# Softmax-minus-one-hot backward: two transfer queues, loads by row or whole block and stores by row, against one queue in a fixed order with even and odd partitions

## The chip, the cores and the metric

The kernel runs on one core of a Trainium2 chip. The metric is the device time of one execution in microseconds (us); the time before is the median of three runs. Logits, labels and the result lie in the chip's main memory (HBM); all arithmetic works on the on-chip memory, which has 128 partitions. Sixteen DMA engines of the core carry data between the two. A transfer (a DMA) is issued by the instruction stream of one engine, here SyncE (SP) or ScalarE (ACT), and goes into that engine's queue; both queues feed the same sixteen DMA engines.

## The reference

The work is the gradient of a cross-entropy loss for 8192 rows of 8192 float32 logits:

```python
logits_max = np.max(logits, axis=-1, keepdims=True)
exp_logits = np.exp(logits - logits_max)
softmax = exp_logits / np.sum(exp_logits, axis=-1, keepdims=True)
one_hot[batch_idx, seq_idx, labels] = 1.0
return (softmax - one_hot).astype(np.float32)
```

Each logit is read once and each result written once: 268.44 MB in and 268.44 MB out.

## The kernel before

**Tiling.** The 8192 rows are cut into 32 blocks of 256 rows. In a block, partition p holds the two neighbouring rows 2p and 2p+1, so what a partition holds of a block is one run of 64 KB in HBM. The first index, j = 0 or 1, of a partition's two rows makes a "row" in the language of the code: row t = 2b + j is the 128x8192 tile of 4 MB with one matrix row per partition. There are 64 such tiles. The buffer `X` has three slots of two tiles each, 8 MB a slot; block b lies in slot b mod 3, and the load of block b+3 must wait until the stores of block b have left the slot.

**Compute.** For each tile, `row_max` lets VectorE (DVE) take the negated maximum of each partition; ScalarE (ACT) computes exp(x - max) in place and sums it; DVE takes the reciprocal of the sum; ACT scales the tile by it; DVE subtracts 1 where a column number (`iota`, held in the matmul memory) equals the label. The order on DVE is written out by hand and staggered by one tile: maximum of tile t+1, then the subtraction of tile t. `finished[t]` names the semaphore count that says that tile t is done. Only the last tile is scaled and subtracted in two halves of 4096 columns.

**Forms of a transfer.** The table `PIECES` names three: "r" moves one tile (128 partitions, one 32 KB run each), "w" a whole block (128 partitions, 64 KB runs), "h" half a block: the 64 even partitions, then the 64 odd ones, both tiles of each, 64 KB runs. The strings `LOADS` and `STORES` choose a form for each block. Before, loads are "r" for blocks 0 to 4 and 26 to 31 and "w" for the 21 blocks between; all stores are "r". "h" is not used. Every helper `run` call records one instruction, so that nearly all instructions stand under line 68 in the profile.

**Order.** `load(b)` issues block b's loads on SP's queue, each waiting for those stores of block b-3 that share its bytes (`meets`); the calls stand in the loop over tiles, one block ahead of the maxima. The last tile of the first three blocks also waits until the column numbers, first made in its place, have been copied away. `store(t)` issues the store of tile t on ACT's queue, after the exponential of tile t+1 and ahead of the scaling of tile t+1. So loads and stores sit in two queues, and each DMA engine has packets of both to serve. At the end ACT waits for the last stores.

Of the kernel before, what the change touches and what calls it, by code (L numbers as in the profile page):

```python
# [8 lines left out]
G = 2  # L9
SLOTS = 3  # L10


LOADS = "rrrrrwwwwwwwwwwwwwwwwwwwwwrrrrrr"
STORES = "rrrrrrrrrrrrrrrrrrrrrrrrrrrrrrrr"


@with_exitstack
def kernel(
    ctx: ExitStack,
    tc: tile.TileContext,  # L20
    logits: bass.AP,
    labels: bass.AP,
    out: bass.AP,
):
    nc = tc.nc
    fp32 = mybir.dt.float32
    i32 = mybir.dt.int32
    i16 = mybir.dt.int16
    Act = mybir.ActivationFunctionType
    Alu = mybir.AluOpType  # L30

    x_nv = logits.flatten_outer_dims()
    o_nv = out.flatten_outer_dims()
    N, V = x_nv.shape
    T = N // P
    B = T // G
    lab_bp = labels.rearrange("a b -> (a b)").rearrange("(b q) -> b q", q=G * P)
    x_b = x_nv.rearrange("(b p j) v -> b p j v", p=P, j=G)
    o_b = o_nv.rearrange("(b p j) v -> b p j v", p=P, j=G)

    const = ctx.enter_context(tc.tile_pool(name="const", bufs=1))
    psum = ctx.enter_context(tc.tile_pool(name="psum", bufs=1, space=bass.MemoryType.PSUM))


    X = const.tile([P, SLOTS, G, V], fp32)
    lab_raw = const.tile([B, G * P], labels.dtype)
    lab_f = const.tile([B, G, P], fp32)
    ident = const.tile([B, B], fp32)
    lab = const.tile([P, G, B], fp32)

    m, s, r = (const.tile([P, T], fp32, name=n) for n in ("m", "s", "r"))

    iota = psum.tile([P, V], i16)
    lab_ps = iota[:].bitcast(fp32)[:, :T].rearrange("p (j b) -> p j b", j=G)

    with tc.tile_critical():  # L56
        sem = tc.alloc_semaphore
        got = [[sem(f"got{i}{q}") for q in range(2)] for i in range(SLOTS)]
        put = [[sem(f"put{i}{q}") for q in range(2)] for i in range(SLOTS)]
        lab_got, dve, act, pe, pool = (sem(n) for n in ("lab_got", "dve", "act", "pe", "pool"))  # L60
        count = {}

        def run(engine, waits, counter, method, **operands):

            waits = list(dict.fromkeys(waits))
            for w in waits[:-1]:
                engine.wait_ge(*w)
            instruction = getattr(engine, method)(**operands)  # L68
            for w in waits[-1:]:
                instruction._wait_ge(*w)  # L70
            step = 16 if method == "dma_start" else 1
            instruction.then_inc(counter, step)
            count[counter.name] = count.get(counter.name, 0) + step
            return counter, count[counter.name]


        w_raw = run(nc.scalar, [], lab_got, "dma_start", out=lab_raw[:], in_=lab_bp)
        w = run(nc.gpsimd, [], pool, "memset", ap=ident[:], constant=0.0)
        w_ident = run(
            nc.gpsimd, [w], pool, "affine_select",  # L80
            out=ident[:], in_=ident[:], compare_op=Alu.not_equal, fill=1.0,
            base=0, pattern=[[-1, B]], channel_multiplier=1,
        )

        made = X[:, SLOTS - 1, G - 1, :].bitcast(i16)[:, :V]
        w_made = run(
            nc.gpsimd, [], pool, "iota", out=made, pattern=[[1, V]], base=0, channel_multiplier=0
        )
        step = mybir.dt.size(labels.dtype) // 4
        lab32 = lab_raw[:].bitcast(i32).rearrange("b (p j s) -> b j p s", j=G, s=step)  # L90
        w_lab = run(nc.vector, [w_raw], dve, "tensor_copy", out=lab_f[:], in_=lab32[:, :, :, 0])
        for j in range(G):
            w = run(
                nc.tensor, [w_ident, w_lab], pe, "transpose",
                out=lab_ps[:, j, :], in_=lab_f[:, j, :], identity=ident[:],
            )
        w_turned = run(nc.vector, [w], dve, "tensor_copy", out=lab[:], in_=lab_ps)
        w_iota = run(
            nc.vector, [w_turned, w_made], dve, "tensor_scalar",
            out=iota[:].bitcast(i32), in0=made.bitcast(i32), scalar1=0, scalar2=None, op0=Alu.bitwise_or,  # L100
        )


        every, rows = slice(0, P), slice(0, G)
        PIECES = {
            "r": [(every, slice(j, j + 1)) for j in range(G)],
            "h": [(slice(i, P, 2), rows) for i in range(2)],
            "w": [(every, rows)],
        }

        def meets(a, b):

            sets = [[set(range(*d.indices(n))) for d, n in zip(p, (P, G))] for p in (a, b)]
            return all(x & y for x, y in zip(*sets))


        loaded, stored, finished = {}, {}, []
        last_made = [((every, slice(G - 1, G)), w_iota)]

        def load(b):  # L120
            loaded[b] = []
            before = stored.get(b - SLOTS, last_made if b == SLOTS - 1 else [])
            for q, piece in enumerate(PIECES[LOADS[b]]):
                ps, js = piece
                free = [w for other, w in before if meets(piece, other)]
                w = run(
                    nc.sync, free, got[b % SLOTS][q], "dma_start",
                    out=X[ps, b % SLOTS, js, :], in_=x_b[b, ps, js, :],
                )
                loaded[b].append((piece, w))  # L130

        def store(t):
            b, j = divmod(t, G)
            stored.setdefault(b, [])
            for q, piece in enumerate(PIECES[STORES[b]]):
                ps, js = piece
                if js.stop != j + 1:
                    continue
                w = run(
                    nc.scalar, [finished[t]], put[b % SLOTS][q], "dma_start",  # L140
                    out=o_b[b, ps, js, :], in_=X[ps, b % SLOTS, js, :],
                )
                stored[b].append((piece, w))


        def row(t):
            return X[:, t // G % SLOTS, t % G, :]

        def row_max(t):
            b, j = divmod(t, G)  # L150
            arrived = [w for piece, w in loaded[b] if meets(piece, (every, slice(j, j + 1)))]
            return run(
                nc.vector, arrived, dve, "tensor_reduce",
                out=m[:, t : t + 1], in_=row(t), axis=mybir.AxisListType.X, op=Alu.max, negate=True,
            )


        load(0)
        w_max = row_max(0)
        for t in range(T):  # L160
            x = row(t)
            label = lab[:, t % G, t // G : t // G + 1]
            w = run(
                nc.scalar, [w_max], act, "activation",
                out=x, in_=x, func=Act.Exp, bias=m[:, t : t + 1], scale=1.0, accum_out=s[:, t : t + 1],
            )
            w_sum = run(nc.vector, [w], dve, "reciprocal", out=r[:, t : t + 1], in_=s[:, t : t + 1])
            if t + 1 < T:
                if (t + 1) % G == 0:
                    load((t + 1) // G)  # L170
                w_max = row_max(t + 1)
            if t > 0:
                store(t - 1)

            n = 1 if t + 1 < T else 2
            cols = [slice(i * V // n, (i + 1) * V // n) for i in range(n)]
            scaled = [
                run(
                    nc.scalar, [w_sum], act, "activation",
                    out=x[:, c], in_=x[:, c], func=Act.Copy, bias=0.0, scale=r[:, t : t + 1],  # L180
                )
                for c in cols
            ]
            for c, w in zip(cols, scaled):
                w = run(
                    nc.vector, [w], dve, "scalar_tensor_tensor",
                    out=x[:, c], in0=iota[:, c], scalar=label, in1=x[:, c],
                    op0=Alu.is_equal, op1=Alu.subtract, reverse1=True,
                )
            finished.append(w)  # L190
        store(T - 1)
        for b in range(B - SLOTS, B):
            for _, w in stored[b]:
                nc.scalar.wait_ge(*w)


# [28 lines left out]
```

## Time and profile before

| what | value |
|---|---|
| median of 3 runs | 1247.56 us (1247.33 to 1247.74) |
| profiled execution, first to last instruction (its span, the only own time that it has) | 1245.7 us |
| median over that span | 1.8 us more |
| DMA over the span | 536.98 MB, mean 431 GB/s |
| busy: DVE, ACT | 1119.2 us (90%), 919.1 us (74%) |
| SP's queue, waiting for stores to land | 446.9 + 699.1 us |
| DVE, waiting for loads | 94.3 us, 25 times |
| stores: issues on ACT's queue | 64, 338 ns each (median) |
| loads: issues on SP's queue | 22 of 4 MB, 21 of 8 MB |

Busy shares are of the span. A row of the profile's busy shares in 40 slices has one digit a slice, 9 for 90% or more. The DMA row is the mean over the sixteen DMA engines, and a busy DMA engine is one that has a packet under way. "Idle before" is time in which an engine waited, with the event that ended it. Windows are stretches of the span in us; a window's GB/s counts whole packets, so in windows of a few us it swings by some per cent.

### The profile page before, as it was taken

The numbers are of one execution on the slowest core, as the hardware profiler recorded it, in microseconds if no ns is written. First come the engines' busy times: TensorE is split into PE (matmuls) and PEld (weight loads), VectorE is DVE, ScalarE is ACT, GpSimd is POOL, SyncE is SP. The second block draws the span as 40 slices with busy tenths as digits, with TensorE's granted clock in tenths as the row PEclk, the third lists the DMA queues.
The fourth block names the chain that finished last, engine by engine and source line by source line (L and its number), as shares of the span: only waits on it lengthen the run. The fifth ranks groups of instructions, "written<-read, shape, count | busy, mean of one in ns | idle before, by whom it ended". The sixth has DMA issues, their size and how long they took to land.

```text
span 1245.7 us, 592 instructions
## 1 busy us (share of the span) xinstructions
PE 0.4 (0%) x2; PEld 0.3 (0%) x2; DVE 1119.2 (90%) x196; ACT 919.1 (74%) x194; POOL 7.4 (1%) x7
## 2 busy tenths in 40 slices
PE   0000000000000000000000000000000000000000
PEld 0000000000000000000000000000000000000000
DVE  5999998888988889888998888988889999999893
ACT  3888886778776787767877778777777788887772
POOL 2000000000000000000000000000000000000000
DMA  9999999999999999999999999999999999999998
GB/s 406 417 429 433 438 433 442 437 426 427 430 435 445 439 417 442 426 430 437 432 443 438 420 435 432 430 437 450 420 426 437 436 428 432 437 435 429 432 437 386
DMA packets 15460, 536.98 MB, mean 431 GB/s; under 512 B 1728, under 2 KB 1728, under 8 KB 1760
## 3 DMA queue, kind: packets, MB, share of 16 engines
q1 hardware_dynamic: 6192, 268.44, 50.0%
q10 hardware_dynamic: 9264, 268.51, 49.9%
q14 instruction: 4, 0.03, 0.0%
HBM read 268.50 MB, written 268.44 MB: 431 GB/s over the span
## 4 chain that ended last, share of the span: by engine, by line
DMA 59%; DVE 37%; another core or an unknown queue 2%; ACT 1%; DVEq 0%; issue 0%; PE 0%; SPq 0%; ACTq 0%
DMA X<-in_logits_dram 31%; DMA out_dram<-X 27%; DVE m L68 18%; DVE X L68 18%; ACT X L68 1%; DVE iota L68 0%; DVEq L56 0%; DMA lab_raw<-in_labels_dram 0%; DVE lab_f L68 0%; DVE r L68 0%; PE iota L68 0%; SPq L68 0%; ACTq L68 0%; DVE lab L68 0%
## 5 line engine op out<-in xcount | busy, mean ns | idle before, releaser
L68 DVE TENSOR_REDUCE m<-X 128x1 f32<-128x8192 f32 x64 | 555.2, 8675 | 94.3 <-DMA X<-in_logits_dram 94.3
L68 ACT ACTIVATE X<-X,m 128x8192 f32<-128x8192 f32 x64 | 455.9, 7123 | 188.4 <-DVE m L68 188.4
L68 DVE SCALAR_TENSOR_TENSOR X<-iota,lab,X 128x8192 f32<-128x8192 int16 (+1 forms) x65 | 559.7, 8612 | 4.1 <-ACT X L68 4.1
L68 ACT ACTIVATE X<-X,r 128x8192 f32<-128x8192 f32 (+1 forms) x65 | 456.0, 7017 | 115.9 <-DVE r L68 115.9
L68 DVE RECIPROCAL r<-s 128x1 f32<-128x1 f32 x64 | 9.9, 154 | 7.3 <-ACT X L68 7.3
L68 ACT ACTIVATION_READ_ACCUMULATOR X<-X,m 128x1 f32 x64 | 12.0, 187 | 0.0
L68 DVE CAST lab_f<-lab_raw 32x256 f32<-32x256 int32 x1 | 3.7, 3685 | 4.7 <-DMA lab_raw<-in_labels_dram 4.7
L68 POOL IOTA X<- 128x8192 int16 x1 | 6.9, 6944 | 0.0
L68 DVE TENSOR_SCALAR iota<-X 128x4096 int32<-128x4096 int32 x1 | 4.4, 4427 | 0.1
L68 ACT ACT_TABLE_LOAD x1 | 1.3, 1283 | 1.3 <-SPq L56 1.3
L68 DVE COPY lab<-iota 128x64 f32<-128x64 f32 x1 | 0.2, 225 | 0.5 <-PE iota L68 0.5
L68 PE MATMUL iota<-ident,lab_f 32*128 32x32 f32 x2 | 0.4, 300 | 8.5 <-DVE lab_f L68 8.5
L68 PEld LDWEIGHTS iota<-ident,lab_f 32*128 32x128 f32 x2 | 0.3, 196 | 8.4 <-DVE lab_f L68 8.4
L68 POOL TENSOR_SCALAR_AFFINE_SELECT ident<-ident 32x32 f32<-32x32 f32 x1 | 0.2, 204 | 0.1
L68 POOL MEMSET ident<- 32x32 f32 x1 | 0.1, 115 | 0.5 <-SPq L56 0.5
L209 POOL MEMSET const-bfloat16-1.0<- 128x1 bf16 x1 | 0.1, 107 | 0.0
L209 POOL MEMSET const-uint8-127<- 128x1 uint8 x1 | 0.1, 107 | 0.0
L209 POOL MEMSET const-float32-0.0<- 128x1 f32 x1 | 0.1, 104 | 0.2 <-issue 0.2
L209 POOL MEMSET const-float32-1.0<- 128x1 f32 x1 | 0.1, 104 | 0.0
## 6 DMA issues: line engine op xcount, KB each, us to landing
out_dram<-X ACTq DMA_DIRECT2D x64, 4096.0 KB, 30.8
X<-in_logits_dram SPq DMA_DIRECT2D x22, 4096.0 KB, 26.6
X<-in_logits_dram SPq DMA_DIRECT2D x21, 33.4
lab_raw<-in_labels_dram ACTq DMA_DIRECT2D x1, 64.0 KB, 3.8
```

The costliest lines, as they stand in the source:

```text
L68: instruction = getattr(engine, method)(**operands)
L209: nc = _bacc.Bacc("TRN2", target_bir_lowering=False, num_devices=1)
```

## The change

All transfers go into SP's queue. A list `transfers` fixes their order: the six pieces of the first three blocks' loads; then, for each block b, the two pieces of its store and the two pieces of the load of block b+3, while there is one. `load` and `store` now issue one piece q. `issue_until_loaded(b)` walks the list until block b's loads have been issued; it is called once for the first three blocks and from `row_max`, and what is left of the list, the last stores, follows after the loop. SP therefore waits, in this order, for what each piece needs: a store for `finished` of the later of the tiles that it holds, a load for the store of the same piece of block b-3.

The forms change too. Loads: "r" for blocks 0 to 3 and 31, "h" for 4 to 30. Stores: "r" for 0, 28 and 31, "h" for 1 to 27, 29 and 30. So 16 transfers move a tile in 32 KB runs and 112 move half a block on 64 partitions in 64 KB runs. Before, 86 moved a tile and 21 a block. On the compute engines nothing moves, but for the 64 store issues that leave ACT's stream; the final wait goes from ACT to SP.

```diff
-LOADS = "rrrrrwwwwwwwwwwwwwwwwwwwwwrrrrrr"
-STORES = "rrrrrrrrrrrrrrrrrrrrrrrrrrrrrrrr"
+LOADS = "rrrr" + 27 * "h" + "r"
+STORES = "r" + 27 * "h" + "r" + "hh" + "r"
...
+        def load(b, q):
+            piece = PIECES[LOADS[b]][q]
+            ps, js = piece
             before = stored.get(b - SLOTS, last_made if b == SLOTS - 1 else [])
...
+            w = run(
+                nc.sync, [w for other, w in before if meets(piece, other)], got[b % SLOTS][q],
+                "dma_start", out=X[ps, b % SLOTS, js, :], in_=x_b[b, ps, js, :],
+            )
+            loaded.setdefault(b, []).append((piece, w))
+
+        def store(b, q):
+            piece = PIECES[STORES[b]][q]
+            ps, js = piece
+            w = run(
+                nc.sync, [finished[b * G + js.stop - 1]], put[b % SLOTS][q],
+                "dma_start", out=o_b[b, ps, js, :], in_=X[ps, b % SLOTS, js, :],
+            )
+            stored.setdefault(b, []).append((piece, w))
+
+        transfers = [(load, b, q) for b in range(SLOTS) for q in range(G)]
+        for b in range(B):
+            transfers += [(store, b, q) for q in range(G)]
+            if b + SLOTS < B:
+                transfers += [(load, b + SLOTS, q) for q in range(G)]
+        transfers = iter(transfers)
+
+        def issue_until_loaded(b):
+            while len(loaded.get(b, [])) < G:
+                move, *which = next(transfers)
+                move(*which)
...
         def row_max(t):
             b, j = divmod(t, G)
+            issue_until_loaded(b)
...
-        load(0)
+        issue_until_loaded(SLOTS - 1)
...
-                if (t + 1) % G == 0:
-                    load((t + 1) // G)
                 w_max = row_max(t + 1)
-            if t > 0:
-                store(t - 1)
...
-        store(T - 1)
+        for move, *which in transfers:
+            move(*which)
         for b in range(B - SLOTS, B):
             for _, w in stored[b]:
-                nc.scalar.wait_ge(*w)
+                nc.sync.wait_ge(*w)
```

## The prediction

> **What bounds the kernel now.** I read the page's slices first (which resource is full all the way), then the waits of the queue and of the engines, then the chain of waits, and last the windows by stage and the DMA queues in them. First the page: the slices, and the queues' packets with the share of the sixteen DMA engines' time.
>
> ```profile
> DVE  5999998888988889888998888988889999999893
> ACT  3888886778776787767877778777777788887772
> DMA  9999999999999999999999999999999999999998
> DMA packets 15460, 536.98 MB, mean 431 GB/s; under 512 B 1728, under 2 KB 1728, under 8 KB 1760
> q1 hardware_dynamic: 6192, 268.44, 50.0%
> q10 hardware_dynamic: 9264, 268.51, 49.9%
> ```
>
> DMA is full in all 40 slices; DVE is not. The two queues together took 99.9% of the DMA engines' time. Next the waits, of SP's queue and of the engines (microseconds, times, longest):
>
> ```profile
> SPq L68 <- DMA out_dram<-X: 699.1, 37, 57.3
> SPq L67 <- DMA out_dram<-X: 446.9, 21, 21.5
> ...
> ACT X L68 <- DVE m L68: 188.4, 64, 19.7
> ACT X L68 <- DVE r L68: 115.9, 64, 2.1
> DVE m L68 <- DMA X<-in_logits_dram: 94.3, 25, 6.9
> ```
>
> SP spends 1146 us waiting for stores to land before it may load; the compute engines wait for data, not the other way round. The chain of waits (start, length) shows the middle's beat:
>
> ```profile
> 192.36 8.69 DVE m L68
> 201.05 8.66 DVE X L68
> ...
> 209.74 27.34 DMA out_dram<-X
> ...
> 966.92 8.69 DVE m L68
> ```
>
> From 192.36 to 966.92 lie 20 blocks: 38.73 us a block, of which DVE works 2 x (8.69 + 8.66) = 34.7 us. So DVE has 4 us to spare in each. Last the windows (stretch, busy time of five engines, clock, DMA share, GB/s), and the queues of a loads-only stretch (6 to 46 us) and of the middle (160 to 960 us):
>
> ```profile
> 48.00:54.00 6.00, 0.00 (x0) 0.00 (x0) 6.00 (x1) 6.00 (x1) 0.00 (x0) 1.00 0.99 344
> 160.00:960.00 800.00, 0.00 (x0) 0.00 (x0) 716.08 (x124) 592.12 (x124) 0.00 (x0) 1.00 1.00 434
> 1205.00:1240.00 35.00, 0.00 (x0) 0.00 (x0) 21.05 (x5) 14.83 (x5) 0.00 (x0) 1.00 1.01 434
> ```
> ```profile
> DMA packets 592, 17.30 MB, mean 433 GB/s; under 512 B 64, under 2 KB 64, under 8 KB 64
> ```
> ```profile
> q1 hardware_dynamic: 2992, 175.11, 50.6%
> q10 hardware_dynamic: 5903, 171.94, 49.8%
> ```
>
> Loads alone run at 433 GB/s, stores alone (1205 to 1240) at 434, both mixed at 434. Only one stretch dips: 344 GB/s from 48 to 54 us, just after ACT's queue gets its first store at 46.98 us. The same bytes at 434 GB/s would take 1237 us of the 1245.7, so nothing that the change does to the compute engines can give more than about 8 us, and most of those are the first 2 us, the dip and the end.
>
> **The change part by part.** The profiled execution's span is 1245.7 us, the median 1247.56, so 1.9 us are added at the end.
>
> *Longer runs.* In the middle, SP's queue (64 KB runs) took 50.6% of 16 x 800 us for 175.11 MB, 36.99 us of a DMA engine per MB; ACT's queue (32 KB runs) 49.8% for 171.94 MB, 37.07. Before, 86 tile transfers moved 360.7 MB in 32 KB runs; after, 16 do, 67.1 MB. So 293.6 MB change to the longer run: 293.6 x 0.087 / 16 = 1.6 us less. The shares are rounded to 0.1%, which is 0.07 us per MB either way for the difference: 0.3 to 2.9 us. I take 1.6.
>
> *One queue for two.* The dip cost 6 x (1 - 344/433) = 1.2 us. It is the only time at which one queue starts beside a full other one; stores alone or loads alone show none. Without a second queue I take it as gone, minus 1.2 us; the other end is that it belongs to the first write, and stays: 0. The 64 store issues of 0.34 us leave ACT (21.6 us), which waited 304 us anyway, and join SP, which waits 1146 us: nothing. Had SP no such waits, they would cost those 21.6 us.
>
> *More transfers.* 107 become 128, each with its completion packets (64 of them in the 592 of the loads-only stretch, which holds 4 transfers). That stretch is 1 GB/s below the mixed one, so a boundary costs at most 40 x 0.0023 / 4 = 0.02 us, 21 of them 0.5 us. I take 0, since the stores-only stretch with its boundaries shows 434.
>
> Here the row comes first and a rule after it. The Trainium skill (DMA: Bandwidth & Descriptors, Anatomy of one DMA) gives a DMA a fixed cost of about 2 us beside its bytes; by that, an estimate, 21 more would cost 42 us. The loads-only stretch at 433 GB/s contradicts it for transfers that queue behind each other, and this sum does not use it.
>
> *Order.* On SP a store that waits for DVE now holds up every load behind it. First place: the store of block 1 waits until DVE has finished row 3, 98.9 us. Ahead of it lie 10 transfers of 4.19 MB; 0 to 46 us moved 46 x 412 GB/s = 19.0 MB, the other 23.0 MB take 53.1 us at 433: the queue runs dry at 99.1. An issue takes 1.2 us until data move (first issue 0.96, first load packets just after 2 us), so between 98.9 + 1.2 and 99.1 lies a hole of 1.0 us; if the dip stays or the first loads are slower than a window of whole packets says, there is none. I take 0.2. Block 2: row 5 done at 133.5, the queue dry at 99.1 + 4 x 9.7 = 138; block 3: 168 against 177. From there the lead grows by 4 us a block until DVE waits for its loads, since 34.7 < 38.7.
>
> *Halves of a block.* A row now waits for both halves of its block, as it did for "w"; stores of a block go when its second tile is done, 17.3 us later than the first's before. In the beat: block b+1 has landed 38.7 us before store b's turn, and row 2b+1 is done 17.3 us into block b+1 (staggered by a tile), so 21 us remain. At the end, with E the landing of the last load: row 61 done at E + 13.3, row 63 at E + 39.3, the turns of their stores at E + 19.4 and E + 48.4. The DMA engines stay full, and the cover is 6 us at its thinnest.
>
> *64 partitions in a transfer.* No load or store of the trace has fewer than 128. Nearest by run length: the 64 KB loads, 36.99 us per MB, no loss. Nearest by partitions: the label load, 32 of them, in 2 KB runs in the first 2 us:
>
> ```profile
> q10 hardware_dynamic: 48, 0.07, 1.8%
> ```
>
> That is 1.8% of 16 x 13 us for 0.07 MB, 53 us per MB, 1.4 times as long. I take no loss: what the sixteen engines' time went into is the bytes of long runs, and in run length and neighbours the label load is far off. Both ends stay: 0, or 40% of 112 x 9.69 = 1085 us, 434 us. Below nothing there is no room, the mixed rate being that of each kind alone.
>
> The skill speaks against this part. DMA: Bandwidth & Descriptors (Rules for kernel authors) says not to split a transfer into disjoint partition halves, since both halves use the same sixteen engines. SBUF — State Buffer (Door 1) says that 64 neighbouring partitions reach 8 of 16 ports; by its formula even partitions reach all 16, but it does not say which engine serves which of them. If two engines met at one port throughout, the middle would run at half rate, an estimate of 1085 us more. No row here shows that.
>
> *Sum:* -1.6 - 1.2 + 0.2 = -2.6 us: span 1243.1, median 1245.0.
>
> **Rivals.** (a) *The forecast's case*, DMA full at one even rate: 1243.0 to 1247, by the ends of the terms. That the change buys nothing measurable (within 0.2%, 2.5 us, about what a measurement can tell here) is the half of it in which the dip stays or the packets give little: 1246.
>
> (b) *64 partitions spread badly.* Place: the 112 half-block pieces, 1085 us. It decides from 0.24% (2.6 us); by the label's row it gives up to 1680 us. For it: the only transfer under 128 partitions is slower. Against: that one's 2 KB runs and its place at the start explain it as well.
>
> (c) *A turn from loads to stores costs.* In one queue, loads and stores alternate in pure stretches of 19 us, and the dip may be the price of such a turn. 29 turns instead of one, 28 x 1.2 = 34 us, less the 1.6: 1279. For it: the dip is the one place where pure loads turn to stores. Against: near 1199.7 us the last load ends and stores go on at 434.
>
> (d) *The order starves the queue* at block 1, 2 and at the end: 1 to 8 us (8: the end's cover of 6 us missing, and the hole), 1246 to 1253. Against: the leads above.
>
> **How the numbers follow.** (a) 0.60, of which 0.40 faster by over 0.2% and 0.20 within; (b) 0.21, slower; (c) 0.13, slower; (d) 0.06, of which 0.04 within and 0.02 slower. Faster 0.40, same 0.24, slower 0.36. The likeliest case's own range is 1243 to 1247; 8 in 10 needs (c) and (d) and the small end of (b), so 1243 to 1281; the rest of (b), 0.16, lies above.
>
> **What would show it.** Right: DMA at 433 to 434 GB/s in every window, no dip near 50 us, a beat of 38.65 to 38.7 us a block, DVE's waits for loads still near 94 us. Wrong: a window of the middle under 430 GB/s; time per MB on the one queue above 37.1 (then b); dips every 38.7 us (then c); DMA under 9 in a slice or SP waiting for DVE beyond the third block (then d).

## The result and the profile after

The changed kernel takes 1251.85 us (median of 5 runs, 1251.29 to 1252.52), beside 1247.74 us (1247.33 to 1248.65) for the kernel before on the same chip: 1.0033 times the time before, 95% interval 1.0022 to 1.0044. It is slower by 4.1 us. The forecast was 1245.0 us, 2.6 us faster, so it missed by 6.9 us and in sign; the time lies in the range given.

The profiled execution has a span of 1250.1 us; the median lies 1.75 us above it, as before (1.8). First the page of the changed kernel: the same slices, and the queue's packets.

```profile
DVE  5999999988899888998888988889888898888993
ACT  3888888777777777777778777687767877778782
DMA  9999999999999999999999999999999999999998
GB/s 405 419 432 424 432 434 436 434 430 424 428 430 436 436 432 436 434 432 436 436 436 434 432 432 430 430 428 436 432 436 436 436 436 436 434 436 419 447 417 350
DMA packets 11317, 536.99 MB, mean 430 GB/s; under 512 B 2064, under 2 KB 2064, under 8 KB 2096
q1 hardware_dynamic: 11264, 536.88, 99.6%
```

The DMA engines are still busy from end to end, and the one queue took 99.6% of their time. So the loss isn't in a queue that stands empty for long; it is in what the packets took, and in the last slices. Next the waits of the engines, and then those of SP's queue.

```profile
DVE m L68 <- DMA X<-in_logits_dram: 98.3, 25, 4.9
```
```profile
SPq L68 <- DMA out_dram<-X: 1006.5, 58, 28.2
SPq L68 <- DVE r L68: 132.6, 8, 33.0
SPq L68 <- DVE X L68: 12.4, 1, 12.4
```

DVE's waits for loads are 98.3 us, as forecast (near 94). SP waits for tiles that DVE has to finish nine times: six in the first 260 us, none from there to 1190 us, three at the end. The chain of waits has the beat of the middle:

```profile
824.55 37.45 DMA out_dram<-X
863.21 37.43 DMA out_dram<-X
901.85 37.45 DMA out_dram<-X
940.51 37.43 DMA out_dram<-X
```

The starts lie 38.66, 38.64 and 38.66 us apart, where the kernel before had 38.73: the beat that was forecast. The windows (stretch, busy time of five engines, clock, DMA share, GB/s) show where that gain went:

```profile
48.00:54.00 6.00, 0.00 (x0) 0.00 (x0) 6.00 (x1) 6.00 (x1) 0.00 (x0) 1.00 0.99 426
56.00:62.00 6.00, 0.00 (x0) 0.00 (x0) 6.00 (x1) 6.00 (x1) 0.00 (x0) 1.00 0.95 355
160.00:960.00 800.00, 0.00 (x0) 0.00 (x0) 721.31 (x126) 599.78 (x126) 0.00 (x0) 1.00 1.00 434
1205.00:1240.00 35.00, 0.00 (x0) 0.00 (x0) 25.08 (x5) 20.57 (x5) 0.00 (x0) 1.00 0.98 424
```

The dip that the prediction took as gone is there, only later: 355 GB/s from 56 to 62 us, where the queue turns from its first loads to its first stores. The middle has 434 GB/s, the end 424 instead of 434. The last windows show one more thing. Of the kernel before:

```profile
1242.00:1244.00 2.00, 0.00 (x0) 0.00 (x0) 0.00 (x0) 0.00 (x0) 0.00 (x0) 1.00 0.27 115
1244.00:1246.00 2.00, 0.00 (x0) 0.00 (x0) 0.00 (x0) 0.00 (x0) 0.00 (x0) 1.00 0.00 0
```

and of the changed kernel:

```profile
1242.00:1244.00 2.00, 0.00 (x0) 0.00 (x0) 0.00 (x0) 0.00 (x0) 0.00 (x0) 1.00 1.22 524
1244.00:1246.00 2.00, 0.00 (x0) 0.00 (x0) 0.00 (x0) 0.00 (x0) 0.00 (x0) 1.00 0.27 115
1246.00:1248.00 2.00, 0.00 (x0) 0.00 (x0) 0.00 (x0) 0.00 (x0) 0.00 (x0) 1.00 0.15 66
```

After 1244 us a few DMA engines work alone. The packet records of the trace tell which: with one queue, the packets that each DMA engine moves follow one another in a known order, so each record can be given to one engine by its start and size. Ten engines finish their last packet at 1244.5 to 1244.6 us, the other six at 1244.9, 1246.1 and 1247.6 to 1248.3. Each transfer has sixteen completion marks in the trace, one for each engine, and the kernel counts it as complete when all sixteen are there (`step = 16`).

The distance between the first and the last engine's completion mark of one transfer ("the spread" from here on) grows like this: 0.3 us at 13 us, 0.5 at 91, 1.3 at 141, 2.3 at 218, 3.8 at 334, 4.3 at 450, 5.3 at 557 and 5.7 from about 720 us on, where it stays until 1204 us. The kernel before is not free of it: its spread is 0.4 to 0.7 us until 236 us, then 0.7 to 2.0 for most transfers and 2.5 to 4.1 for the others, and 2.1 for the last one (marks from 1242.4 to 1244.5 us). In the changed kernel the last one has 3.8 (1244.8 to 1248.6): of the 4.1 us between the last marks, 1.7 are added spread, and by the other 2.4 even the first engine is later.

It grows at one kind of place. A 64 KB packet takes 2418 ns, a 32 KB packet 1213 ns (medians). What exceeds that after the first 55 us, 61 us over all engines, lies mostly (51 us) in the last two load packets ahead of a turn from loads to stores, up to 1.4 us each. A turn from stores to loads costs nothing, but for one: the last store packets of block 1, near 120 us, take 0.3 to 0.7 us more on ten engines. The first turn (58 to 62 us) costs every engine 0.5 to 1.0 us, the turn near 140 us (the load of block 4 to the store of block 2) 0.7 to 2.0 us. Between 300 and 760 us the ten leading engines lose next to nothing (0.3 us at most), and the six others 1.0 to 3.2 us each; after 760 us nobody loses more than 0.6 us.

### The profile page after: what moved, and what is told of

Same layout as the page of the kernel before. It is cut to its first block, busy times and chain, and to the rows that moved or that the text cites. A ratio compares the mean times of both kernels' runs of the same rounds, so it can differ in the third digit from the quotient of the medians.

```text
span 1250.1 us, 646 instructions
## 1 busy us (share of the span) xinstructions
PE 0.4 (0%) x2; PEld 0.3 (0%) x2; DVE 1116.5 (89%) x196; ACT 919.0 (74%) x194; POOL 7.4 (1%) x7
## 3 DMA queue, kind: packets, MB, share of 16 engines
q1 hardware_dynamic: 11264, 536.88, 99.6%
## 4 chain that ended last, share of the span: by engine, by line
DMA 74%; DVE 21%; SPq 2%; ACT 1%; issue 1%; PE 0%; ACTq 0%; DVEq 0%
DMA out_dram<-X 72%; DVE m L68 10%; DVE X L68 10%; SPq L68 2%; DMA X<-in_logits_dram 2%; ACT X L68 1%; DMA lab_raw<-in_labels_dram 1%; DVE iota L68 0%; DVE r L68 0%; DVE lab_f L68 0%; PE iota L68 0%; DVE lab L68 0%; ACTq L224 0%; DVEq L67 0%; SPq L56 0%
## 5 line engine op out<-in xcount | busy, mean ns | idle before, releaser
L68 DVE TENSOR_REDUCE m<-X 128x1 f32<-128x8192 f32 x64 | 555.2, 8675 | 98.3 <-DMA X<-in_logits_dram 98.3
L68 DVE CAST lab_f<-lab_raw 32x256 f32<-32x256 int32 x1 | 1.0, 993 | 7.4 <-DMA lab_raw<-in_labels_dram 7.4
## 6 DMA issues: line engine op xcount, KB each, us to landing
X<-in_logits_dram SPq DMA_DIRECT2D x54, 19.3
```

## The experiments

Two theories stood at the start. One: the turns from loads to stores in the one queue set engines back, and the kernel waits for the last engine. The other: the half-block transfers on 64 partitions, or the compute engines' own traffic and waits, put engines out of step, and the turns only show it. The kernel before, run beside each group of kernels, took 1247.30 us (beside the changed kernel once more, all by row, more turns in the changed kernel's forms, and two queues both ways), 1247.61 us (beside the transfers without compute, more turns in rows, and each direction alone) and 1247.94 us (beside 11 turns and one turn). Ratios are to these.

**The changed kernel once more**

> The changed kernel once more, for a second profile. In its first profile six of the sixteen DMA engines lost up to 1.4 us each time in the last load packet ahead of a store, and the last engine finished 3.8 us behind the first. Turn theory (in one queue, a turn from loads to stores costs the last load packet up to 1.4 us on some engines, and these stay behind): the same packets are slow again, 5 to 7 engines end 2 to 4 us late, 1251 to 1253 us. Chance theory (single slow packets anywhere): other packets are slow, and the time moves by more than 1 us. Form theory (64 partitions in a transfer load the DMA engines unevenly): the same engines, slow packets anywhere in half-block pieces.

1251.71 us (1249.91 to 1252.12), ratio 1.0032 (1.0021 to 1.0043). The slow packets lie at the same place: 28.1 us over all engines in 70 packets that are the last ahead of a turn, and 10.4 in 17 packets one ahead of these. Eight engines are behind this time instead of six, and the ends lie between 1242.6 and 1246.3 us, in a profiled execution with a span of 1248.1 us: 3.7 us apart at the end, about as in the first execution (3.8), but the whole 2 us earlier. (This execution, at 1249.91 us, is the fastest of the seven.) How many engines fall behind, and how far, differs between executions of one kernel. Here the spread stops at 4.0 us instead of 5.7, and the stretch in which the first execution's queue ran empty is full. First the first execution, then this one:

```profile
1200.00:1212.00 12.00, 0.00 (x0) 0.00 (x0) 12.00 (x3) 9.54 (x3) 0.00 (x0) 1.00 0.89 382
1200.00:1212.00 12.00, 0.00 (x0) 0.00 (x0) 12.00 (x4) 9.03 (x4) 0.00 (x0) 1.00 1.01 437
```

**All transfers by row in the one queue.** No transfer has fewer than 128 partitions:

```diff
-LOADS = "rrrr" + 27 * "h" + "r"
-STORES = "r" + 27 * "h" + "r" + "hh" + "r"
+LOADS = 32 * "r"
+STORES = 32 * "r"
```

> The changed kernel, one queue and fixed order, but every transfer by row (128 partitions, 32 KB runs). Turn theory: the same 29 turns, so engines fall behind as before, plus up to 1.6 us for the shorter runs: 1251 to 1254 us. Form theory: no 64-partition transfer is left, so the loss goes: 1245 to 1248.5 us.

1253.33 us (1252.58 to 1254.17), ratio 1.0046 (1.0031 to 1.0061). Windows of this kernel:

```profile
160.00:960.00 800.00, 0.00 (x0) 0.00 (x0) 730.35 (x127) 603.65 (x127) 0.00 (x0) 1.00 1.00 432
1244.00:1246.00 2.00, 0.00 (x0) 0.00 (x0) 0.00 (x0) 0.00 (x0) 0.00 (x0) 1.00 0.38 164
1246.00:1248.00 2.00, 0.00 (x0) 0.00 (x0) 0.00 (x0) 0.00 (x0) 0.00 (x0) 1.00 0.15 66
```

The engines' ends spread from 1243.1 to 1249.0 us, with the slow packets again the last ones of the second load (19.3 us over all engines in the last, 13.0 in the one ahead of it). So the 64 partitions and the forms are not the cause. Against the changed kernel this one is 1.6 us slower (1253.33 - 1251.71), what the prediction gave for the longer runs, though the intervals of the two ratios overlap.

**The transfers without the compute**

```diff
         def store(b, q):
 ...
-                nc.sync, [finished[b * G + js.stop - 1]], put[b % SLOTS][q],
+                nc.sync, [w for other, w in loaded[b] if meets(piece, other)], put[b % SLOTS][q],
```

The loop over the tiles is left out, too, so what is stored is the logits as they were loaded.

> The changed kernel's transfers, waits between slots and order on the one queue, with the compute left out (no maximum, exponential, scaling or subtraction; it writes the logits back), so that a store is issued as soon as its block has landed. Lead theory (the turn from loads to stores costs where the store has been in the queue for some time with few transfers ahead of it; a store issued just in time or far behind others costs nothing on the engines that run in step): the first store is issued near 23 us with four loads ahead, so the turn near 62 us costs under 0.3 us an engine where it cost 0.8; a few engines still fall behind at later turns; 1244 to 1250 us. Compute theory (the compute engines' use of the on-chip memory slows the last load packet): no slow packets at any turn, 1242 to 1244 us. Plain turn theory (each turn costs): as the changed kernel at every turn, 1249 to 1253 us.

1250.32 us (1248.90 to 1250.95), ratio to the kernel before 1.0021 (1.0011 to 1.0030). Windows (ACT does nothing in the copies and has no column):

```profile
30.00:60.00 30.00, 0.00 (x0) 0.00 (x0) 0.00 (x0) 0.00 (x0) 1.00 1.01 419
1242.00:1244.00 2.00, 0.00 (x0) 0.00 (x0) 0.00 (x0) 0.00 (x0) 1.00 0.42 180
1244.00:1246.00 2.00, 0.00 (x0) 0.00 (x0) 0.00 (x0) 0.00 (x0) 1.00 0.08 33
```

With DVE and ACT idle, ten engines end at 1241.2 to 1241.8 and six at 1243.3 to 1246.9 us. So the compute engines and the waits for them don't cause the spread; they can cost the changed kernel no more than the 1.4 us between 1250.3 and 1251.7. A place for these 1.4 us shows in the packets: in the changed kernel the three transfers that end between 120 and 142 us (the second store of block 1 and the loads of block 4) took 25.6 us too long over all engines, 1.3 to 2.5 on each, and here the same three took 0.2. By row, with the compute, they took about 0.5. One idea fell here: that a turn is cheap when its store is issued long ahead. No store here waits for anything but its load, and the first turn still cost every engine 0.9 to 1.25 us.

**Three blocks loaded, then three stored: 11 turns, not 30.** From the transfers without compute:

```diff
-        transfers = [(load, b, q) for b in range(SLOTS) for q in range(G)]
-        for b in range(B):
-            transfers += [(store, b, q) for q in range(G)]
-            if b + SLOTS < B:
-                transfers += [(load, b + SLOTS, q) for q in range(G)]
+        transfers = []
+        for b in range(0, B, SLOTS):
+            group = range(b, min(b + SLOTS, B))
+            transfers += [(load, x, q) for x in group for q in range(G)]
+            transfers += [(store, x, q) for x in group for q in range(G)]
```

> The transfers alone, on SP's one queue in the same forms as the changed kernel, but three blocks are loaded and then those three are stored: 11 turns from loads to stores where the changed kernel's order has 30. The compute is left out, so the blocks are stored as they were loaded. If each turn puts some engines a little further behind (the first, at 62 us of copy_only, cost 0.9 to 1.25 us on every engine and the spread of the ends there grew to 5.75 us over the turns up to about 700 us, some 0.35 us a turn), a third of the turns should leave a spread of 2 to 4 us and a time of 1245 to 1249 us. If engines drift apart under one queue or under these forms whatever the order, the spread is again 5 to 6 us and the time 1249 to 1251 us, as copy_only's 1250.3.

1248.34 us (1247.35 to 1248.69), ratio to the kernel before 1.0003 (0.9993 to 1.0013). Windows:

```profile
30.00:60.00 30.00, 0.00 (x0) 0.00 (x0) 0.00 (x0) 0.00 (x0) 1.00 0.99 419
1242.00:1244.00 2.00, 0.00 (x0) 0.00 (x0) 0.00 (x0) 0.00 (x0) 1.00 0.15 66
1244.00:1246.00 2.00, 0.00 (x0) 0.00 (x0) 0.00 (x0) 0.00 (x0) 1.00 0.00 0
```

The ends spread from 1241.6 to 1244.5 us, 2.9 us. The first turn cost 1.2 us an engine on the mean (0.8 to 1.5), the second nothing, the others up to 0.4 us on the mean.

**All loads, then all stores: one turn.** From the transfers without compute. The waits change with the order: a load waits for the load, not the store, of the block three before it, and every store reads one of the last three blocks:

```diff
-            before = stored.get(b - SLOTS, last_made if b == SLOTS - 1 else [])
+            before = loaded.get(b - SLOTS, last_made if b == SLOTS - 1 else [])
...
-                nc.sync, [w for other, w in loaded[b] if meets(piece, other)], put[b % SLOTS][q],
+                nc.sync, [w for other, w in loaded[B - SLOTS + (b - B + SLOTS) % SLOTS] if meets(piece, other)], put[b % SLOTS][q],
...
-        transfers = [(load, b, q) for b in range(SLOTS) for q in range(G)]
-        for b in range(B):
-            transfers += [(store, b, q) for q in range(G)]
-            if b + SLOTS < B:
-                transfers += [(load, b + SLOTS, q) for q in range(G)]
+        transfers = [(load, b, q) for b in range(B) for q in range(G)]
+        transfers += [(store, b, q) for b in range(B) for q in range(G)]
```

> The transfers alone again, on the one queue and in the same forms, but all loads first and then all stores: one turn. The compute is left out, and later blocks overwrite earlier ones unstored, so this moves the same bytes and nothing else. If the turns are what sets engines back: one turn, 1 to 1.5 us on every engine, a spread of the ends under 1.5 us, and 1242 to 1246 us by the packet times of mixed traffic (a stretch of loads alone or stores alone may have packet times of its own, which this run shows). If one queue or the forms make engines drift without turns: a spread of 5 to 6 us and 1249 to 1251 us.

1246.01 us (1245.69 to 1246.35), ratio to the kernel before 0.9985 (0.9975 to 0.9994). Windows:

```profile
30.00:60.00 30.00, 0.00 (x0) 0.00 (x0) 0.00 (x0) 0.00 (x0) 1.00 1.01 437
618.00:624.00 6.00, 0.00 (x0) 0.00 (x0) 0.00 (x0) 0.00 (x0) 1.00 1.02 437
1240.00:1242.00 2.00, 0.00 (x0) 0.00 (x0) 0.00 (x0) 0.00 (x0) 1.00 0.04 16
1242.00:1244.00 2.00, 0.00 (x0) 0.00 (x0) 0.00 (x0) 0.00 (x0) 1.00 0.00 0
```

Loads go on from 30 to 60 us, and there is no dip: 437 GB/s where the two copies that turn to stores there have 419. So the dip needs the turn at that place; the turn near 620 us has none (437 GB/s from 618 to 624 us). Until 600 us the spread stays under 0.5 us; fifteen engines end at 1240.8 to 1241.2 and one at 1242.3 us. The three copies differ in the order alone, and in the waits that go with it: 1, 11 and 30 turns give spreads of 1.5, 2.9 and 5.7 us and times of 1246.0, 1248.3 and 1250.3 us. The theory of one queue or the forms as such, which gave 1249 to 1251 us for 1 and 11 turns too, falls. The single turn itself, though, cost no last load packet more than a few tens of ns on fifteen engines, and one packet 0.4 us on the sixteenth, against the 1 to 1.5 us that were expected.

**More turns: from block 6 on, half a load and half a store by turns**, 53 turns from loads to stores instead of 30 (the expectations count 52). In the changed kernel's forms, and in rows:

```diff
-            transfers += [(store, b, q) for q in range(G)]
+            if b <= 6 or b + SLOTS > B:
+                transfers += [(store, b, q) for q in range(G)]
             if b + SLOTS < B:
-                transfers += [(load, b + SLOTS, q) for q in range(G)]
+                for q in range(G):
+                    transfers.append((load, b + SLOTS, q))
+                    if b >= 6:
+                        transfers.append((store, b + 1, q))
```

> The changed kernel, one queue, but from block 6 on load and store pieces alternate one by one (load half, store half) instead of two by two: twice as many turns from loads to stores in the middle, 52 in all for 29. Turn theory: the last engine loses about twice as much in the middle, 4 to 6 us more than the changed kernel: 1255 to 1258 us. Form theory, and any theory that puts the loss on the start or the end of the order: as the changed kernel, 1250.5 to 1253 us.

> One queue, every transfer by row, and from block 6 on loads and stores alternate one by one. A row's store is known long before its turn, so the queue stays three to four transfers deep, other than with half-block pieces in this order, where the store of the first half was issued 1.1 us before its turn, the engines fell into step there, and each pair of turns cost about 2 us. Lead theory: deep queue, engines in step pay nothing, some fall behind; 1250 to 1258 us. Plain turn theory: 52 turns at 1 to 2 us, 1275 to 1300 us.

In rows: 1251.98 us (1251.70 to 1253.73), ratio 1.0036 (1.0023 to 1.0049), the ends from 1243.2 to 1249.0 us, and the middle as full as with 30 turns:

```profile
160.00:960.00 800.00, 0.00 (x0) 0.00 (x0) 732.50 (x127) 604.23 (x127) 0.00 (x0) 1.00 1.00 433
```

So the loss doesn't go on growing with the turns: it stops near 5.9 us, and a fixed price per turn is refuted. In the changed kernel's forms: 1296.43 us (1294.92 to 1297.17), ratio 1.0393 (1.0376 to 1.0411), for a reason of its own:

```profile
160.00:300.00 140.00, 0.00 (x0) 0.00 (x0) 131.21 (x24) 113.37 (x24) 0.00 (x0) 1.00 1.00 431
365.00:600.00 235.00, 0.00 (x0) 0.00 (x0) 200.03 (x35) 165.22 (x35) 0.00 (x0) 1.00 1.01 415
600.00:960.00 360.00, 0.00 (x0) 0.00 (x0) 305.88 (x54) 257.03 (x54) 0.00 (x0) 1.00 1.00 411
```

The turns between 307 and 355 us were free. A half-block store needs both rows of its block done, and at 365 us it came too late for its turn: the queue ran dry. From then on the store of the first half was issued only just ahead of its turn (at 404.71 us for packets from 405.8), the engines were in step within about 1 us, and every pair of turns cost about 0.6 us in the last store packets and 1.1 to 1.45 us in the last load packets, on the mean over the sixteen engines. The mechanism that was expected was wrong here; what the run shows is that in this kernel turns were dear to all engines from the moment at which the queue held little ahead of them. That the short queue makes them dear isn't shown.

**Two queues with the changed kernel's forms**, all on the kernel before:

```diff
-LOADS = "rrrrrwwwwwwwwwwwwwwwwwwwwwrrrrrr"
-STORES = "rrrrrrrrrrrrrrrrrrrrrrrrrrrrrrrr"
+LOADS = "rrrr" + 27 * "h" + "r"
+STORES = "r" + 27 * "h" + "r" + "hh" + "r"
```

> The kernel before with its two queues, but with the changed kernel's forms (even and odd partitions in 64 KB runs for the middle blocks, both ways). Turn theory: loads and stores mix packet by packet in two queues, so there is no pure turn; no engine falls behind by more than the 2.1 us of before, and the time is that of before or up to 1.6 us less: 1245.5 to 1248 us. Form theory: engines fall behind as in the changed kernel, 1251 to 1254 us.

1289.92 us (1287.76 to 1291.46), ratio 1.0338 (1.0322 to 1.0353): far above what was expected. Windows:

```profile
376.00:384.00 8.00, 0.00 (x0) 0.00 (x0) 8.00 (x3) 5.69 (x1) 0.00 (x0) 1.00 0.94 328
384.00:452.00 68.00, 0.00 (x0) 0.00 (x0) 57.85 (x11) 48.16 (x11) 0.00 (x0) 1.00 1.00 432
160.00:960.00 800.00, 0.00 (x0) 0.00 (x0) 693.59 (x121) 570.56 (x121) 0.00 (x0) 1.00 0.99 417
```

The stores of a block now go out in pairs. Between the pairs ACT's queue runs empty and loads run alone; when a pair starts (377.14 us here), the rate drops to 328 GB/s for 8 us, about 2 us lost, and so again every second block. That looks like the dip of 48 to 54 us of the kernel before, again and again: stores that start after a stretch of loads alone. Ten such dips between 160 and 960 us make about 20 of the 31 us that 417 instead of 434 GB/s mean there; the rest isn't assigned. In the kernel before rows are stored one by one, and its trace has one such dip.

Each direction alone, in two queues: loads "h" with stores by row, and loads as before with stores "h".

> The kernel before, two queues, stores by row, but the middle blocks' loads as even, then odd partitions. Dry-queue theory (with stores as pairs on a second queue, that queue runs dry, and each start of a store beside loads alone costs about 2 us; in the run with both forms changed this was seen every second block): stores by row keep the second queue filled, so no such starts, 1246 to 1250 us. Form theory (64-partition pieces are slow when loads and stores mix): 1265 to 1290 us.

> The kernel before, two queues, loads as they were, but stores as in the changed kernel (middle blocks as even, then odd partitions, both once the second row is done). Dry-queue theory: the store queue runs dry between pairs, starts beside loads alone cost about 2 us each, 1270 to 1295 us. Form theory: about half of the 42 us that both forms cost together, 1260 to 1275 us.

Half-block loads alone: 1262.13 us (1261.58 to 1263.86), ratio 1.0116 (1.0101 to 1.0131), as neither theory had it. Windows:

```profile
160.00:960.00 800.00, 0.00 (x0) 0.00 (x0) 717.31 (x125) 588.61 (x124) 0.00 (x0) 1.00 1.00 433
1200.00:1262.00 62.00, 0.00 (x0) 0.00 (x0) 45.61 (x10) 36.62 (x10) 0.00 (x0) 1.00 0.74 316
```

The middle is full at 433 GB/s; the loss is nearly all at the end, where loads reach DVE later: the last subtraction starts at 1240.8 us, before at 1221.3, and the DMA engines have too little left to do. Half-block stores alone: 1377.18 us (1374.45 to 1382.87), ratio 1.1042 (1.1015 to 1.1069), more than either theory gave. Its window, and its wait of DVE for loads in the list of waits:

```profile
160.00:960.00 800.00, 0.00 (x0) 0.00 (x0) 634.88 (x112) 523.40 (x110) 0.00 (x0) 1.00 0.94 383
```
```profile
DVE m L68 <- DMA X<-in_logits_dram: 225.6, 26, 16.1
```

The DMA share is 0.94, so engines stand empty: by the code, a whole-block load must wait for both stores of a late pair. Both runs bear on how the forms and two queues fit each other, and tell little about the turn.

## Why the prediction was wrong

*The step that failed* is "One queue for two", minus 1.2 us. It took the dip as a price of a second queue that starts beside a full one. The dip stayed (355 GB/s from 56 to 62 us; 0.8 us an engine on the mean), and the copy with one turn shows that it comes with the turn from loads to stores there: where loads go on, 30 to 60 us have 437 GB/s, against 419. The other end that the step kept, that the dip belongs to the first write and stays, was the nearer one, but not enough; and in that copy the first write, near 620 us, has no dip. With it fell what the sum took as given without a term, that the sixteen DMA engines stay in step: in the copies they end 1.5, 2.9 and 5.7 us apart with 1, 11 and 30 turns, and the kernel waits for the last.

*Rival (c), a turn from loads to stores costs,* had the right kind of mechanism and the wrong size: 1.2 us on every engine at each of 28 turns, 34 us (it counted 29 turns; the order has 30). The engines pay about 2 us each for the first and the third turn together; from then on mainly those pay that are behind already, until they are some 5.7 us late. Its sign of dips every 38.7 us didn't show, because the leaders keep the beat at 38.65 us and the middle's window hides six engines that slip. Nor did its witness against, that stores go on at 434 GB/s after the last load, speak against it: by then turns cost nothing any more.

*The sum against the trace.* Forecast span 1243.1, measured 1250.1 us: 6.9 more before rounding. The forecast was taken from the span before, which holds a spread of 2.1 us at its end; now it is 3.8, so 1.7 us are added spread. The leaders' last mark would have come at 1239.8 (1242.4 - 2.6) and came at 1244.8: 5.0 us later. Of these, 0.5 lie in the first load, which landed at 13.2 instead of 12.7 us, about 2.2 in slow packets between 55 and 145 us, 0.1 in those after that, and 1.4 to 1.8 in the empty queue at the end; some 0.5 us are not assigned. The last 0.2 us lie behind the last mark.

*Order.* The hole of 1.0 us at block 1, taken as 0.2, did not appear: its store was issued at 98.9 us, as worked out, and data went on without a gap. The cover of 6 us at the end was what the skew used up. The working had one E for all engines; the last load lands between 1184.86 (first engine) and 1190.58 us (last). Row 61 is done 13.3 us after the last of these, at 1203.8, but the leaders' turn comes 19.4 us after the first, at 1204.3. The issue takes 1.2 us until data move, so ten engines stood empty for 0.7 to 1.3 us there, and again, for less, at the store of block 31. This was (d)'s place, reached through (c)'s cause: in the second execution, with a spread of 4.0 us, the queue did not run empty there, and all ends came 2 us earlier. (d)'s other sign, SP waiting for DVE beyond the third block, showed as well (six waits in 260 us), but there the queue stayed full. That the time fell into the range, and into (d)'s 1246 to 1253, is luck in the main: the range was wide for (b)'s and (c)'s sake, and (d) had no engines that fall behind.

*Longer runs.* Minus 1.6 us: the beat fell from 38.73 to 38.65 us, and by row the one queue is 1.6 us slower than in halves (intervals of the two ratios overlap). *More transfers:* 21 more cost nothing that shows; the leaders' beat has no room for it. The 2 us for each transfer, which the prediction quotes from the Trainium skill (DMA: Bandwidth & Descriptors, Anatomy of one DMA) and does not use, stand there for transfers issued from GpSimd; those here are issued from SP and ACT. *64 partitions:* no loss. Rival (b), to which the prediction gave 0.21, is out: the rate of the middle is 434 GB/s in these transfers, as was argued from run length against the label load's row. The advice against partition halves in the Trainium skill (DMA: Bandwidth & Descriptors, Rules for kernel authors) did not turn into a loss here: halves in one queue ran 0.1% faster than rows, which is within the noise.

*What stays open:* why the first turn cost every engine, the copy's single turn at 620 us none; why the transfers around the third turn cost every engine in the changed kernel, but not without its compute and not by row; why, later, the leaders go free; and why the lag stops at 5.7 us. The runs show where and how much, not by what mechanism in the DMA engine. Nor was it tried to stop the lag in the changed kernel itself; that three slots of the buffer leave no order with fewer turns in which DVE always has a block to work on is an argument, and no run shows it.

## What to carry to other kernels

A copy-bound kernel ends with its last DMA engine, so sixteen engines at "99.6% busy" can hide several us: look at the spread of the completion marks of one transfer, and at the last windows, not only at the mean rate. In these runs, loads and stores that alternate in long stretches lost time where loads turn to stores, if not at every turn, in one queue and, as it seems, in two of which one runs empty; two queues that both always hold work, as in the kernel before, had one such place. When a dip has a single occurrence in a trace, list what else was first at that moment before its cause is taken as removed.

## What the runs showed that was not expected

- A load packet next to a turn to stores takes up to 1.4 us more than its 2418 ns (64 KB) or 1213 ns (32 KB), and up to 1.8 in the run of 53 turns in halves; a store packet ahead of a load does not, except at 120 us in the changed kernel (up to 0.7 us) and in that run (0.6 us).
- The DMA engines of one queue are not held together: they drifted to 5.7 us apart and stayed so for over 400 us, and every transfer was complete that much later than its first engine's part.
- With the order reduced to one turn, the transfers without compute take 1246.0 us, only 1.9 us less than the kernel before with all its compute (1247.9): there is little left to win by the order of these transfers.
- Two queues with half-block forms cost 38 us more than one queue with the same forms (1289.9 against 1251.7): the forms that are harmless in one queue let the store queue run empty in two, which accounts for part of it.
